# Low parts of attention keys beside rows of zeros: score products over 128 rows instead of 64

## Chip, cores and metric

The kernel runs on one core of a Trainium2 chip, in one launch. The metric is the device time of one execution in microseconds (us). A core has five engines with queues of their own that run in order: TensorE (PE, with its weight loader PEld), VectorE (DVE), ScalarE (ACT), GpSimd (POOL) and SyncE (SP, which issues the transfers).

## What is computed

A network for 256 tokens of width 1024, in float32. Block one has two layers of feed-forward, token mixing, feed-forward; block two has two layers of a hybrid of three attentions followed by an MLP. The change touches two kinds of scores. In token mixing, families A (banded attention) and C (stick-breaking attention), six heads each:

```
scores = jnp.einsum('bnqhd,bnkhd->bhnqk', qc, kband) * (d ** -0.5)     # A, d = 64
z = jnp.einsum('bqhd,bkhd->bhqk', q[:, q0:kend], k[:, :kend]) * scale  # C, d = 64
```

In the hybrid, sparse attention ("nsa") with eight heads in two groups, over compressed, selected and window keys:

```
s_c = jnp.einsum('bgrqd,bgnd->bgrqn', qb, k_cmp)
s_s = jnp.einsum('bgrqd,bgqnld->bgrqnl', qb, k_g)
p_w = masked_softmax(jnp.einsum('bgrqd,bgkd->bgrqk', qb, kwb), mask_w)
```

## The kernel before

Float32 accuracy is reached with split operands: x = H + L, where H is x rounded to the TensorE's fast float32 format and L the rest. A product of two split operands is H·H + H·L + L·H. The weights stream through three raw tiles; ACT writes H, DVE (POOL when DVE is behind) writes L into a ring of six tiles `hl`, and the TensorE takes them from there. The stages run one after the other: feed-forward, mixing, feed-forward for each layer, then hybrid and MLP for each layer. Attention work is laid into the same queues between the weight products.

The order on every engine is fixed when the program is built. `Sched` keeps a clock per engine from a cost per instruction and always issues the instruction that could start first; a task (a generator) waits for tiles from pools (`Slots`) or for flags. A matmul's cost there includes a model of the TensorE's activity, which counts columns times rows (`cols` in `mm`, L546 is the line at which all instructions are issued). All records of the trace therefore carry line L546; instructions are told apart by their tiles.

The scores of a head have 64 rows of contraction (the head's width), half of the 128 rows of the array. Two heads share a tile: head 0 on rows 0 to 63, head 1 on rows 64 to 127. `qk_post` writes for each head x a query tile with H of the query on its own rows and L on the other half, and a key tile `kst` of three planes: plane x has H of the key on all 128 rows, and plane 2 has L of both keys, each on its own rows. `scores` then makes two products per head and token tile: one over 128 rows (H and L of the query times H of the key), and one over 64 rows (H of the query times L of the key):

```
yield self.mm(o, q[:, i, c], k[:, i], seg == 0, False, ...)
yield self.mm(o, q[r, i, c], k[r, 2], False, True, ...)
```

Family C adds the mask with a product by the identity (`identb`, `cb`, bfloat16). In block two `keys` and `nsa_pair` do the same with `kc` (tile `kcat`, H) and `kl` (L, in the place of tile `tA`); `qT` lies in `hlq`. Per layer there are 4 pairs of heads, 2 groups and 3 pairs of products. `nsa_qk` sets the columns behind the keys to zero, `nsa_pair` reads gates from `gate24`. The memory attention (`mem_head`, tiles `hlk` and `hlq`) has heads of 128, so its three products per score are over 128 rows.

Of the kernel before, what the change touches and what calls it, by code (L numbers as in the profile page):

```python
# [45 lines left out]
# ---------------------------------------------------------------- weights  # L46
# The main stream reads the weights in the order of use, in "halves":
# [128, 1024] float32, what one step multiplies with all 256 tokens.

def ws_half(w, c0):  # L50
    """Columns c0:c0+128 of a [1024, n] matrix: [128 p, 8 k, 128 c]."""
    return w[:, c0:c0 + 128].reshape(8, 128, 128).transpose(1, 0, 2).reshape(128, 1024)


def ts_halves(w, cols, per=2):
    """Columns of a [1024, n] matrix, per row chunks of 128 in a half: [128 p, per, n]."""
    a = w[:, cols]
    n = a.shape[1]
    a = a.reshape(8 // per, per, 128, n).transpose(0, 2, 1, 3).reshape(8 // per, 128, per * n)
    if per * n < 1024:  # L60
        a = np.concatenate([a, np.zeros((8 // per, 128, 1024 - per * n), np.float32)], -1)
    return list(a)
# [59 lines left out]
def merge_order(b):  # L122
    """Gates (None, j) and branch halves (i, None) of a branch."""
    if b == 0:
        return [(None, j) for j in range(8)] + [(i, None) for i in range(4)]
    return [u for i in range(4) for u in ((None, 2 * i), (None, 2 * i + 1), (i, None))]
# [56 lines left out]
# ---------------------------------------------------------------- constants of the shapes  # L183
# [9 lines left out]
def constants():  # L193
# [25 lines left out]
    # decay sums: E[tok] = sum over a range of tokens, as columns of 0 or -1/16  # L219
# [10 lines left out]
    # order F, 1, 2, 4, B, 64, 32, 16, 8  # L230

    # predicates for A^T[j, i] of the levels that are computed whole: i = j, and 1, 2, 4, 8
# [13 lines left out]
def prepare(inp, stages):  # L246
# [15 lines left out]
    # block two: per-partition columns of gains, and rows that are broadcast  # L262
# [13 lines left out]
# ---------------------------------------------------------------- the kernel  # L276

class Slots:
    """Tiles that are handed out and returned; a task yields (slots) or (slots, n) to get some."""
# [23 lines left out]
class Op:  # L303
    """One instruction, not yet issued."""
# [12 lines left out]
def region(a):  # L317
    """(name, in PSUM, partitions, elements of a partition) that an operand covers; whole banks of PSUM."""
# [28 lines left out]
class Engine:  # L347
    """Makes the instructions of one engine."""
# [58 lines left out]
class Sched:  # L407
    """Lists the instructions of all tasks in one order: the one that can start first by the engines'
    clocks is issued first. A task is a generator of instructions (Op), of conditions to wait for
    (a function) and of requests for tiles (Slots, or (Slots, n))."""  # L410
# [19 lines left out]
    def step(self, t):  # L430
        """Runs a task up to its next instruction, or until it has to wait."""
# [54 lines left out]
    def stream(self, s, cost, cols):  # L486
        """The end of a matmul that starts at s: the array runs at half its clock in a period that follows
        one of little activity."""
# [120 lines left out]
class Prog:  # L609
# [41 lines left out]
    # ---- small helpers  # L651
# [21 lines left out]
    def mm3(self, out, l, r, start=True, stop=True):  # L673
        """Product of split operands: l(hl), r(hl) give the parts."""
# [6 lines left out]
    def gain(self, ap):  # L681
        """A gain [1024] on every partition, in a scratch tile."""
        g = yield self.scr
        yield self.bcast(g, ap, D)
        return g
# [5 lines left out]
    def hl_gain(self, H, L, src, g):  # L691
        """Split of src * g, g a column or a number."""
# [3 lines left out]
    def chunk(self, src):  # L696
        """A split [128, 256] operand for the main stream."""
# [4 lines left out]
    # ---- weights: loaded and split ahead of the main stream  # L702
# [45 lines left out]
    def pooled(self, low):  # L748
        """Takes what the vector engine falls behind with."""
# [22 lines left out]
    # ---- norms  # L772
    def rstd(self, st, a, b, n):
        """(sum of columns a and b of st + n eps)^-0.5, in place of a."""
# [5 lines left out]
    def norm(self, t, x, Gn, dst, st):  # L780
        """dst[:, k, t, hl, :] = rms(x) * gain of token tile t, transposed and split. Gn: the gain times 32."""
# [31 lines left out]
    # ---- matrix products of the main stream  # L813
    def ws_mm(self, p, w, act, nk=8, off=0, parts=1):
        """Weights stationary. One part: [128 columns, 256]; two, which value() adds: [128 columns, t, hl, 128]."""
# [19 lines left out]
    def ws_first(self, n, done):  # L835
        """The first n products of a stage: those of the first tile of tokens ahead of the others."""
# [23 lines left out]
    def ws_unit(self, parts=1):  # L860
        """One product of the main stream: (result, where it goes back to, parts)."""
# [6 lines left out]
    def value(self, pr):  # L868
        """A product as one [128, 256] operand, and the tile that holds it if there is one."""
# [19 lines left out]
    def ts_bank(self, y, w, c, t, first, last, **kw):  # L889
        """y += tokens of tile t times a chunk w(hl) of weights; c: [128, t, hl, 128]."""  # L890
# [3 lines left out]
    def ts_mm(self, y, w, c, t, first):  # L894
        """y [128, 2, 512] += tokens of tile t times w [128, 1024]."""
# [4 lines left out]
    def ts_group(self, width, split=False):  # L900
        """All tokens times a group of columns: a pair of banks, tokens of a tile in each."""
# [22 lines left out]
    # ---- the end of a stage: the last chunks, residual, next norm  # L924
    def gains(self, post, after):
        """The gains for the end of a stage: that of its result, times 32 and the residual's factor, and the next one's, times 32."""
# [9 lines left out]
    def finish(self, chunks, names, ys, post, after, fills):  # L936
        """The last chunks (by name) of a stage; ys: the banks of the tiles of tokens."""
# [63 lines left out]
    def give_gain(self, name):  # L1001
        """Both tiles of tokens are through with a gain."""
# [5 lines left out]
    # ---- memory: keys and values of both layers, in the gaps between the stages  # L1008
# [16 lines left out]
    def fill(self, f):  # L1025
        """256 columns of the memory's keys (f%4 < 2) or values."""
# [22 lines left out]
    def mem_keys(self, l, c, p, y):  # L1049
        """Normed keys of two heads, transposed: memk[:, head, memory token]."""  # L1050
# [17 lines left out]
    # ---- the feed-forward networks  # L1068
# [71 lines left out]
    # ---- token mixing of block one  # L1140
# [15 lines left out]
    def table(self, name):  # L1156
        """The functions of the next stage, once this one's are done with."""
# [3 lines left out]
    def qk_post(self, l, it, pr, qk):  # L1161
# [9 lines left out]
        else:  # L1171
            # of each of two heads: queries with the high parts on its rows and the low ones on the others;
            # keys with the high parts on all rows, and the low ones on its own
# [4 lines left out]
            for r, o, x in HALVES:  # L1178
                yield nc.vector.scalar_tensor_tensor(t2[r, 2] if what == "k" else t2[o, x], src[r], sc,
# [49 lines left out]
    def scores(self, s, q, k, rows, stacked, strict=False):  # L1229
        """s: a bank [128 q, (q1: 256 keys | q0: 256 keys)] for each of two row groups."""  # L1230
        for i, r in enumerate(rows):
            for seg, t in ((0, 1), (1, 0)):
                o = s[i][:, seg * 256:(seg + 1) * 256]
                c = slice(t * 128, (t + 1) * 128)
                if stacked:
                    yield self.mm(o, q[:, i, c], k[:, i], seg == 0, False, skip_group_check=seg > 0)
                    yield self.mm(o, q[r, i, c], k[r, 2], False, True, skip_group_check=seg > 0)
# [7 lines left out]
    def smax(self, Pt, s, biases):  # L1245
        """Exponentials of biased scores of two maps: P [128, 2, 384], and their sums in st[:, :, 2:4]."""
# [15 lines left out]
    def pv_t(self, Tt, Ps):  # L1262
        """Transposed probabilities [128 k, n, (k0: q0 q1 | k1: q1)] of maps [128 q, (q1: k0 k1 | q0: k0)]."""
# [14 lines left out]
    def pv_mm(self, p, T, col):  # L1278
        """o^T [128 = 2 heads x 64, 256 tokens]; V columns col, col+64."""
# [38 lines left out]
    def att_b(self, j, q, k):  # L1318
# [33 lines left out]
        # r = (mean of the squares of a head + eps)^-0.5 on every partition of the head  # L1352
# [42 lines left out]
    # ---- block two  # L1395
    def setup2(self, p2):
# [12 lines left out]
        self.gate24 = t2([128, 2, 24], "gate24")  # L1409
# [17 lines left out]
    def rope_tables(self):  # L1427
        nc, a = self.nc, self.a
        # cos and sin of position * frequency: [128, 3, 8] (two token tiles, block ends)
# [24 lines left out]
    def again(self, tag, shape, dt=FT):  # L1454
        """A new tile in the place of the last one of a tag."""
# [7 lines left out]
    def rope(self, x, cos, sin, shape):  # L1463
        """Rotates the first 16 of the last axis of x [.., 64] in place."""
# [18 lines left out]
    def head_norm(self, x, p, nt, nh, d, gs, times=1.0):  # L1483
        """x [p, nt, nh, d] in place: rms over d, gains (view of x, gain) or none, times a factor."""
# [59 lines left out]
    def cmp_post(self, v, pr):  # L1544
        """The windows of compressed keys or values: 2 x 16 positions of each, split."""
# [55 lines left out]
    def hyb(self, l, after, fills):  # L1601
        nc, a = self.nc, self.a
        self.done &= {"dec"}
        self.tA, self.tB = (self.again(n, [128, 2, w])[:, :, :512] for n, w in (("tA", 512), ("tB", 768)))
# [4 lines left out]
        # gates, low-rank gate, memory queries, gla values  # L1609
# [27 lines left out]
        # merge  # L1637
# [39 lines left out]
    # ---- memory attention  # L1677
# [60 lines left out]
    # ---- gated linear attention  # L1738
    def gla_gate(self, l):
        """sp = -log sigmoid of the gates, per token, split: [128 tokens, hl, t, 256]."""  # L1740
# [27 lines left out]
    def gla(self):  # L1768
        nc, gq, gr, gv = self.nc, self.gq, self.gr, self.tB
        och = self.och[1] = {}  # L1770
        for half in range(2):
# [6 lines left out]
            for t in range(2):  # L1778
# [14 lines left out]
                # slots: t0: 1 2 4 B | 64 32 16 8, t1: F 1 2 4 | 64 32 16 8  # L1793
# [36 lines left out]
            # o [tokens, dv] of both heads, normed, then transposed  # L1830
# [41 lines left out]
    # ---- nsa: queries, keys, then the three branches  # L1872
    def nsa_qk(self):
# [17 lines left out]
        # of a row group g: rows 64g.. the high parts, the other rows the low parts  # L1891
# [14 lines left out]
        kl = self.again("tA", [128, 2, 512], FR).rearrange("p a c -> p (a c)")[:, :528]  # L1906
        yield nc.vector.memset(kc[:, :, 256:272].bitcast(FT), 0.0)
        yield nc.vector.memset(kl[:, 256:272].bitcast(FT), 0.0)
# [14 lines left out]
    def split_v(self):  # L1923
        yield lambda: ("o", 1) in self.done
        # a token tile, kind: 64 values of the first group, zeros, 64 of the second
# [7 lines left out]
    def keys(self, src, view):  # L1933
        """The high parts of the keys of a row group on all rows, and the low parts on its own."""
# [4 lines left out]
        for r, o, x in HALVES:  # L1939
            yield nc.vector.tensor_sub(view(kl[r]), src[r], view(kc[r, x]).bitcast(FT))  # L1940

    def cmp_tail(self, v, pb):
        """Compressed keys or values: gelu, second product, and for keys norm, rotation, transposition."""
# [47 lines left out]
    def nsa_pair(self, j, qT, kv, och):  # L1991
        """Heads j and j+4 (rows 0-63 and 64-127)."""
# [203 lines left out]
```

## Time and profile before

| | |
|---|---|
| median of 3 runs | 2043.14 us (2041.13 to 2045.71) |
| profiled execution: span, first to last instruction | 2040.8 us |
| own time of the profiled execution | not listed apart from the three runs; its span lies 2.3 us below their median |
| TensorE busy | 1995.6 us, 98% |
| weight loads busy | 1732.3 us, 85% |
| DVE, ACT, POOL busy | 1424.7 us (70%), 1205.0 us (59%), 267.7 us (13%) |
| mean granted TensorE clock | 0.994 |
| transfers | 353.77 MB, mean 173 GB/s |

Busy is the share of time in which an engine has an instruction in flight. TensorE's matmuls overlap: one starts while the one before is still in flight, and ends are modelled. How fast they run is therefore read from the starts, in the timeline: the start of a group, the start of the next, and the count between them. In the names, `b<-kst,qk 64*128 64x256` is a product into a bank `b` of a key `kst` and a query `qk`, weights 64 rows by 128 columns, moving operand 64 rows by 256 columns. PEld rows are the loads of the weights.

### The profile page before, as it was taken

The page shows a single profiled execution, that of the slowest core. Times are in us where ns is not written, and L with a number is a line of the kernel's source. Part 1 is how long each engine was busy: PE and PEld are TensorE (multiplying, and loading weights), DVE is VectorE, ACT ScalarE, POOL GpSimd, SP SyncE. Part 2 cuts the span into 40 slices and gives each one's busy share as a digit, 9 for nine tenths or more (in the row PEclk, how much of TensorE's full clock was granted, in tenths as well). Part 3 has the DMA queues.
Part 4 walks back from the last instruction along what each step waited for, and adds up shares of the span by engine and source line. Part 5 has one row for each costly group of instructions (what it writes and reads, how often), then busy time and mean ns, then how long its engine had stood idle before and what let it go on. Part 6 is the DMA issues. An engine that isn't in the chain of part 4 may idle for free. (4 is left out here: it accounts for less than half of the span.)

```text
span 2040.8 us, 31877 instructions
## 1 busy us (share of the span) xinstructions
PE 1995.6 (98%) x11942; PEld 1732.3 (85%) x11942; DVE 1424.7 (70%) x2525; ACT 1205.0 (59%) x2328; POOL 267.7 (13%) x311
## 2 busy tenths in 40 slices
PE   8999999999999999999999999999999999999999
PEld 7888777888888887788889888998888978898887
DVE  6666887666776678776668777666667787667665
ACT  6655775655565568665556656655555656655553
POOL 1000302000200030020003132310001232411000
PEclk9999999999999999999999999999999999999999
DMA  6655344655665644455565544355565544335553
GB/s 218 222 192 199 117 152 146 215 193 188 208 198 192 206 156 135 167 176 190 187 206 193 173 146 135 102 167 183 192 198 189 165 148 142 114 130 191 188 194 124
DMA packets 100561, 353.77 MB, mean 173 GB/s; under 512 B 12435, under 2 KB 13493, under 8 KB 100406
## 3 DMA queue, kind: packets, MB, share of 16 engines
q1 hardware_dynamic: 100406, 351.74, 52.2%
q8 instruction: 93, 1.52, 0.3%
q14 instruction: 62, 0.51, 0.1%
HBM read 350.64 MB, written 1.05 MB: 172 GB/s over the span
## 5 line engine op out<-in xcount | busy, mean ns | idle before, releaser
L546 PE MATMUL m<-hT,hl 128*128 128x256 f32 (+1 forms) x5856 | 976.4, 322 | 7.7 <-DVE hT L546 7.0
L546 PEld LDWEIGHTS m<-hT,hl 128*128 128x128 f32 x5856 | 853.6, 189 | 104.1 <-DVE hT L546 9.6
L546 ACT CAST hl<-raw 128x1024 fp32r<-128x1024 f32 (+1 forms) x690 | 671.4, 982 | 380.3 <-PE b L546 141.3
L546 DVE TENSOR_TENSOR hl<-raw,hl 128x1024 fp32r<-128x1024 f32 (+1 forms) x641 | 755.5, 1184 | 200.1 <-ACT hl L546 193.1
L546 PE MATMUL b<-hl,chunk 128*128 128x512 f32 x2208 | 517.0, 390 | 0.0
L546 PEld LDWEIGHTS b<-hl,chunk 128*128 128x128 f32 x2208 | 408.9, 188 | 81.8 <-issue 0.7
L546 DVE TENSOR_TENSOR mid<-m,lo 128x256 f32<-128x256 f32 x256 | 108.5, 424 | 221.8 <-ACT lo L546 221.3
L546 PE MATMUL b<-hl,hT 128*128 128x512 f32 (+2 forms) x672 | 149.4, 371 | 0.5 <-DVE hT L546 0.5
L546 ACT CAST chunk<-mid 128x256 fp32r<-128x256 f32 x152 | 61.7, 406 | 120.8 <-DVE mid L546 120.4
L546 POOL TENSOR_SCALAR scr<-scr 128x1024 f32<-128x1024 f32 x17 | 21.1, 1239 | 834.9 <-DMA scr<-ffn_post_g 451.6
L546 PEld LDWEIGHTS b<-hl,hT 128*128 128x128 f32 x672 | 115.9, 188 | 16.6 <-DVE hT L546 0.8
L546 POOL TENSOR_TENSOR hl<-raw,hl 128x256 fp32r<-128x256 f32 x104 | 103.0, 1017 | 192.0 <-ACT hl L546 155.1
L546 ACT COPY lo<-m 128x256 f32<-128x256 f32 x256 | 95.0, 371 | 23.8 <-PE m L546 22.7
L546 PE MATMUL b<-ident,scr 128*128 128x128 f32 (+2 forms) x458 | 78.3, 284 | 17.8 <-DVE scr L546 14.0
L546 PE MATMUL m<-chunk,hl 128*128 128x256 f32 x576 | 82.4, 292 | 0.0
L546 PEld LDWEIGHTS b<-ident,scr 128*128 128x128 f32 (+2 forms) x458 | 54.3, 143 | 33.0 <-DVE scr L546 20.3
L546 PEld LDWEIGHTS m<-chunk,hl 128*128 128x128 f32 x576 | 74.3, 195 | 3.0 <-ACT scr L546 0.7
L546 ACT ACTIVATE scr<-scr,sts 128x16 f32<-128x16 f32 (+2 forms) x152 | 62.8, 415 | 9.4 <-DVE sts L546 9.1
L546 DVE TENSOR_TENSOR chunk<-mid,chunk 128x256 fp32r<-128x256 f32 x152 | 65.3, 430 | 2.3 <-ACT chunk L546 2.0
L546 POOL TENSOR_SCALAR scr<-scr,sts 128x128 f32<-128x128 f32 (+2 forms) x96 | 55.9, 602 | 79.3 <-DVE sts L546 52.1
L546 ACT COPY scr<-b 16x16 f32<-16x16 f32 (+6 forms) x148 | 35.4, 239 | 41.2 <-PE b L546 33.5
L546 ACT ACTIVATE mid<-mid 128x256 f32<-128x256 f32 x88 | 36.7, 417 | 34.1 <-DVE mid L546 34.1
(204 smaller groups left out, 1622.4 us busy)
## 6 DMA issues: line engine op xcount, KB each, us to landing
raw<-w SPq DMA_DIRECT2D x636, 512.0 KB, 3.4
scr<-mem SPq DMA_DIRECT2D x4, 512.0 KB, 6.2
scr<-ffn_post_g SPq DMA_DIRECT2D x4, 512.0 KB, 5.0
bias<-bias SPq DMA_DIRECT2D x6, 256.0 KB, 3.6
scr<-ffn_pre_g SPq DMA_DIRECT2D x3, 512.0 KB, 5.9
scr<-mem_norm SPq DMA_DIRECT2D x2, 512.0 KB, 4.9
scr<-mix_pre_g SPq DMA_DIRECT2D x2, 512.0 KB, 4.2
bias<-alibi SPq DMA_DIRECT2D x4, 256.0 KB, 4.3
```

The costliest lines, as they stand in the source:

```text
L546: r = op.call(*op.args, **op.kw) if op.call is not None else None
```

## The change

Each head gets a plane for the low parts of its key as wide as the array: L on the head's own rows, zeros on the other half. The low product then takes the whole query tile (H and L) and this plane; L of the query meets the zeros. The value is the same. In block one the key tile has four planes instead of three, and there are three such tiles instead of four; the zero halves are written once, at the start, on POOL, and stay. In block two `kl` gets a plane per group (528 columns each) and is set to zero as a whole by DVE at the place where 16 columns were. The tile `tA` grows from 512 to 528 columns a plane, and `gate24` becomes the first 24 columns of `gl` instead of a tile of its own. Comments are gone too, so line numbers move.

```diff
@@ qk_post
             for r, o, x in HALVES:
-                yield nc.vector.scalar_tensor_tensor(t2[r, 2] if what == "k" else t2[o, x], src[r], sc,
+                yield nc.vector.scalar_tensor_tensor(t2[r, 2 + x] if what == "k" else t2[o, x], src[r], sc,
                                                      t2[r, x].bitcast(FT), op0=OP.mult, op1=OP.subtract)
@@ scores
                     yield self.mm(o, q[:, i, c], k[:, i], seg == 0, False, skip_group_check=seg > 0)
-                    yield self.mm(o, q[r, i, c], k[r, 2], False, True, skip_group_check=seg > 0)
+                    yield self.mm(o, q[:, i, c], k[:, 2 + i], False, True, skip_group_check=seg > 0)
@@ setup2
-        self.gate24 = t2([128, 2, 24], "gate24")
+        self.gate24 = self.gl[:, :, 0:24]
@@ hyb
-        self.tA, self.tB = (self.again(n, [128, 2, w])[:, :, :512] for n, w in (("tA", 512), ("tB", 768)))
+        self.tA, self.tB = (self.again(n, [128, 2, w])[:, :, :512] for n, w in (("tA", 528), ("tB", 768)))
@@ nsa_qk
-        kl = self.again("tA", [128, 2, 512], FR).rearrange("p a c -> p (a c)")[:, :528]
+        kl = self.again("tA", [128, 2, 528], FR)
         yield nc.vector.memset(kc[:, :, 256:272].bitcast(FT), 0.0)
-        yield nc.vector.memset(kl[:, 256:272].bitcast(FT), 0.0)
+        yield nc.vector.memset(kl.bitcast(FT), 0.0)
@@ keys
-            yield nc.vector.tensor_sub(view(kl[r]), src[r], view(kc[r, x]).bitcast(FT))
+            yield nc.vector.tensor_sub(view(kl[r, x]), src[r], view(kc[r, x]).bitcast(FT))
@@ nsa_pair
                 yield self.mm(u[:, :n], qT[:, g, j, tq], kc[:, g, c:c + n], True, False)
-                yield self.mm(u[:, :n], qT[r, g, j, tq], kl[r, c:c + n], False, True)
+                yield self.mm(u[:, :n], qT[:, g, j, tq], kl[:, g, c:c + n], False, True)
@@ main
-                self.kst = Slots(p1, "kst", 4, [128, 3, 256], FR)
+                self.kst = Slots(p1, "kst", 3, [128, 4, 256], FR)
...
+                for t in self.kst.free:
+                    for r, o, x in HALVES:
+                        yield nc.gpsimd.memset(t[o, 2 + x].bitcast(FT), 0.0)
```

The order of the instructions on TensorE, at the first scores of family A (`kst` is the key tile, `qk` the query, `b` the bank; - is before, + is now; sizes are those of the results):

```order
 L546 MATMUL m_64<-hT,hl_96 128x2x128
 L546 MATMUL m_63<-hT,hl_97 128x512 x7
-L546 MATMUL b_65<-kst_142,qk_134 128x256 x4
-L546 MATMUL b_70<-kst_142,qk_134 128x256 x4
+L546 MATMUL b_65<-kst_139,qk_134 128x256 x4
+L546 MATMUL b_70<-kst_139,qk_134 128x256 x4
 L546 MATMUL m_63<-hT,hl_97 128x512
 L546 MATMUL m_63<-hT,hl_97 128x2x128 x8
```

The eight products stand where they stood; only the key tile is another of the pool. It is so in all of TensorE's queue. On POOL, at the start of the program (`small` holds the sums for the first norm):

```order
+L546 MEMSET kst_139 64x256 x2
+L546 MEMSET kst_140 64x256 x2
+L546 MEMSET kst_141 64x256 x2
 L546 ISA
 L546 TENSOR_TENSOR small_108<-small_108,mhalf 128x1
```

Six memsets are new ahead of POOL's first work. On DVE, in the sparse attention of the first layer (`hlq` queries, `kcat` and `tA` keys, `hl` a weight half):

```order
 L546 TENSOR_TENSOR hlq<-b_65,hlq 64x512 x2
 L546 MEMSET kcat 128x2x16
-L546 MEMSET tA 128x16
+L546 MEMSET tA 128x1056
 L546 TENSOR_TENSOR hl_96<-raw_95,hl_96 128x1024
 L546 TENSOR_TENSOR tA<-b_66,kcat 64x15 x2
```

The memset keeps its place and grows.

## Rows read from the trace of the kernel before

**Rows 1.** The page: TensorE's busy time, and its clock in 40 slices.

```profile
PE 1995.6 (98%) x11942; PEld 1732.3 (85%) x11942; DVE 1424.7 (70%) x2525; ACT 1205.0 (59%) x2328; POOL 267.7 (13%) x311
PEclk9999999999999999999999999999999999999999
```

**Rows 2.** Stretches: us, then each engine's busy time (instructions), clock, DMA share, GB/s.

```profile
223.00:258.00 35.00, 35.00 (x203) 28.69 (x202) 28.66 (x47) 29.76 (x57) 0.00 (x0) 1.00 0.44 146
285.00:325.00 40.00, 40.00 (x204) 30.59 (x202) 30.05 (x86) 28.42 (x71) 0.59 (x3) 1.00 0.49 162
1238.00:1274.00 36.00, 34.56 (x255) 30.27 (x253) 26.89 (x95) 25.01 (x81) 11.83 (x20) 1.00 0.38 131
```

**Rows 3.** TensorE's waits, 223 to 325, then 1238 to 1310: total us, times, longest.

```profile
PE b L546 <- DVE chunk L546: 1.0, 1, 1.0
...
PE b L546 <- POOL scr L546: 1.4, 1, 1.4
```

**Rows 4.** Groups by shape, products, then loads: count, busy us, mean ns, idle before.

```profile
L546 PE MATMUL b<-kst,qk 64*128 64x256 f32 x48 | 18.3, 381 | 0.0
L546 PE MATMUL b<-kst,qk 128*128 128x256 f32 x48 | 17.0, 355 | 0.0
...
L546 PEld LDWEIGHTS b<-tA,hlq 64*128 64x128 f32 x48 | 8.8, 183 | 6.4 <-issue 0.2
```

**Rows 5.** Timeline of TensorE from 286 us (family A): start us, us, what, count.

```profile
286.06 2.10 PE L546 MATMUL m<-hT,hl 128*128 128x256 f32 x8
287.99 2.47 PE L546 MATMUL b<-kst,qk 128*128 128x256 f32 x8
290.39 0.50 PE L546 MATMUL m<-hT,hl 128*128 128x512 f32 x1
```

**Rows 6.** Timeline of TensorE from 1120.5 us: scores of the memory attention.

```profile
1120.98 1.84 PE L546 MATMUL b<-hlk,hlq 128*128 128x256 f32 x14
1122.66 0.51 PE L546 MATMUL m<-hT,hl 128*128 128x256 f32 x3
```

**Rows 7.** Timeline of the weight loads from 286 us; [idle before <- released by].

```profile
286.03 1.69 PEld L546 LDWEIGHTS m<-hT,hl 128*128 128x128 f32 x8
287.76 0.19 PEld L546 LDWEIGHTS b<-kst,qk 128*128 128x128 f32 x1
288.20 2.06 PEld L546 LDWEIGHTS b<-kst,qk 64*128 64x128 f32 x7 [0.25 <-issue]
```

**Rows 8.** Timeline of TensorE from 1257 us, behind scores of the sparse attention.

```profile
1257.83 2.88 PE L546 MATMUL m<-hT,hl 128*128 128x256 f32 x22
1260.55 0.64 PE L546 MATMUL m<-chunk,hl 128*128 128x256 f32 x4
```

**Rows 9.** Timeline of TensorE from 229.2 us (family C): a mask product and its successor.

```profile
232.50 0.28 PE L546 MATMUL b<-cb,identb 128*128 128x256 bf16 x1
232.54 0.72 PE L546 MATMUL m<-hT,hl 128*128 128x512 f32 x3
```

**Rows 10.** Timeline of POOL: its first work, and a memset in the mixing stage.

```profile
5.96 0.56 POOL L546 TENSOR_TENSOR small<-small,mhalf 128x1 f32<-128x1 f32 x1 [5.52 <-DVE small L546]
...
303.00 0.20 POOL L546 MEMSET bias<- 64x128 f32 x1 [8.18 <-DMA bias<-bias]
```

**Rows 11.** Timeline of DVE from 1238 us: the memset and what follows.

```profile
1238.75 0.07 DVE L546 MEMSET tA<- 128x16 f32 x1
1238.85 1.23 DVE L546 TENSOR_TENSOR hl<-raw,hl 128x1024 fp32r<-128x1024 f32 x1
...
1240.32 0.36 DVE L546 TENSOR_TENSOR tA<-b,kcat 64x15 fp32r<-64x15 f32 x2 [0.24 <-ACT kcat L546]
...
1242.09 1.72 DVE L546 COPY_PREDICATED scr<-pred,b 128x128 f32<-128x128 uint8 x5 [1.42 <-ACT scr L546]
```

**Rows 12.** Timeline of ACT: writes of the first and the fourth key.

```profile
227.33 0.42 ACT L546 ACTIVATE kst<-mid 64x256 fp32r<-64x256 f32 x1
...
282.60 0.42 ACT L546 ACTIVATE kst<-mid 64x256 fp32r<-64x256 f32 x1
```

More of the change, by code (lines that the diff above doesn't have):

```diff
@@ L1999, in nsa_pair @@
         for g in range(2):
-            r = HALVES[g][0]
             sb = yield self.b, 3
```

## Prediction

> **What bounds the kernel now.** I read the page first. TensorE is busy 98% of the span and its granted clock stands at nine tenths or more of the upper level (2.4 GHz) in all 40 slices [rows 1], so only time taken off TensorE's own queue, or off its few waits, can shorten the run. Then the table by stretches, laid over the two places where the changed products run: the mixing stages of block one, at 223 to 325 us and again at 756 to 858, and the sparse attention of block two, at 1238 to 1310 and again at 1716 to 1788. There TensorE is full, at an undisturbed clock of 1.00; the next engines, ACT and DVE, stand at 29.76 and 28.66 of 35 us in the tightest stretch [rows 2]. Third, who waits: in the whole first mixing stage TensorE waits 1.0 us (for DVE), in one sparse attention 1.4 us (for POOL) [rows 3]. So TensorE is the bound in both places, with ACT close behind it at 85%.
>
> Last, the instructions themselves. "Busy" says nothing about the speed of one product, because TensorE's rows overlap; the distance from start to start does. A block of eight score products runs from 287.99 to 290.39: 2.40 us, 0.300 us each [rows 5]. The closest relative with all 128 rows in every operand, the score products of the memory attention (also split in three, also 256 columns, also into one bank), runs 14 products from 1120.98 to 1122.66: 0.120 us each [rows 6]. The weight loads say why. While products of 128 rows follow each other, each load is made while the product before it still runs: eight loads from 286.03 to 287.76, beside the eight products from 286.06 to 287.99 [rows 5, 7]. At the step from a load of 128 rows to one of 64 rows the loader stands still for 0.25 us and is released by nothing that the profile shows [rows 7]. Each block alternates between 128 and 64 rows, so it pays this at every product. That is the stall which the change can take away: not the half-empty array, but the alternation.
>
> **The change, part by part.**
>
> (1) *Widened products.* No product is added or taken away; on TensorE the order is the same and only names of key buffers differ. 96 products of 64 rows (48 in block one, 48 in block two [rows 4]) become products of 128 rows. Each narrow product has two borders, one into it and one out of it. Price of a border: the block of eight has eight (four in, four out). It costs 2.40 us against 8 x 0.120 = 0.96, so 1.44 too much. The bill doesn't end with the block: the first product behind it has a late load too. Behind a block in block two, 22 products take 1257.83 to 1260.55 = 2.72 us instead of 22 x 0.120 = 2.64 [rows 8], 0.08 more. So 1.52 us for eight borders, 0.19 us each. 192 borders x 0.19 = 36.5 us. One correction: the 12 mask products (bfloat16, one per head of family C and layer), which stand behind narrow ones, are followed after only 0.04 us [rows 9] where a plain product takes 0.12; so 12 x 0.08 = 1 us of the border is not there to be saved. That leaves 35.5 us, all on TensorE's own queue, where nothing hides it. Bounds for a widened product, which the trace of before does not show: 0.120 us (the relative) and 0.300 us (as now). I take the relative, since it is the same operation at the same width.
>
> The Trainium skill has a rule that would speak against this. Its page "TensorE: Matmul & The Clock Gate", section "Part 3: Packing small matmuls — row/col tiling", says that a weight load overlaps a running product only where the two use different row groups; by that rule widening would make every load collide and the saving would be nothing (a rival below). The trace disagrees for full rows: the loads of 128 rows above keep up with products of 128 rows.
>
> (2) *What is late next.* A faster TensorE asks for its operands sooner. In the stretch 223 to 258 about 12 narrow products give back 24 x 0.19 = 4.6 us less 0.5 us for six masks, 4.1 us; TensorE then needs 30.9 us and ACT 29.8, 96%. I let 1 us of that be lost in each of the two layers. In 285 to 325 TensorE goes from 40.0 to 35.4 and DVE stays at 30.1: covered. In block two TensorE gives back 48 borders x 0.19 = 9.1 us a layer out of 72; DVE is at 26.9 of 36 and ACT at 25.0, both covered, but the one wait for POOL (1.4 us) can grow, since less work stands between scores and the transposes behind them. I let 0.5 us be lost per layer. Sum of the losses 2 x 1 + 2 x 0.5 = 3 us.
>
> (3) *Zeros for block one.* Six memsets of 64x256 on POOL at the start. A memset of 64x128 took 0.20 us [rows 10], so 0.40 each, 2.4 us in all (bounds 0.2 and 2.4). They stand at the head of POOL's queue, whose first work begins at 5.96 us after an idle time of 5.52 us. Hidden; without that cover 2.4 us, once.
>
> (4) *Zeros for block two.* DVE's memset before the keys grows from 16 to 1056 columns, twice in the run. 16 columns took 0.07 us; an operation of 1024 columns on DVE at this place takes 1.23 us [rows 11]. Between these I take 0.9 us. Behind it stand one weight half and the low parts of the keys; just before and after these DVE waits 0.24 and 1.42 us for ACT, which takes up the 0.9 [rows 11]. Cost nothing; without that cover 2 x 0.9 = 1.8 us.
>
> (5) *Three key tiles in place of four.* The first of a stage's keys is written from 227.33 us on and the fourth from 282.60 [rows 12]. With three tiles the fourth takes the first one's place, and the first one's scores end with the mask product at 232.50 [rows 9], 50 us before. Nothing. The gates that move into another tile's columns keep their operations and their order: nothing. (The lower bound of (3) to (5) is nothing, since none of them takes work away.)
>
> **Sum.** 35.5 - 3 = 32.5, rounded to 32 us. The profiled execution spans 2040.8 us, the median of the runs is 2043.1; the 2.3 us around the span I leave as they are. 2043.1 - 32 = 2011 us.
>
> **Rivals.**
>
> A. *The other engines take over.* The borders vanish, but ACT's in-order queue in block one and the chain scores, DVE, ACT, POOL, transposes in block two already pace the work. For it: ACT at 85%, the wait for POOL. Against it: TensorE waits only 1.0 and 1.4 us in 100 and 72 us. Then 223 to 258 gives nothing (2 x 4.1 = 8.2 lost) and each of the four head pairs of a layer in block two loses what one block of six saves, 6 x 0.19 = 1.1 us (8 x 1.1 = 9 lost): gain 35.5 - 17 = 18, time 2025.
>
> B. *No gain: it is not the row count.* The loader's 0.25 us could belong to something else that score products share, say that every load collides with the product before it in the same rows, or two products into one bank. For it: the profile names no releaser. Against it: the memory attention has all of this and runs at 0.120. Time 2043, within 2 us. This is where the page's rule would lead.
>
> C. *Slower: rows cost array time.* A product's time could grow with its rows; then 96 products take twice their 0.12 us, and where blocks border on other narrow work the stall stays. It decides once a widened product passes the 0.300 us of now: 96 x 0.12 = 11.5 us more and no stall saved, 2055. Against it: nothing in the profile makes a 128-row product longer than a 64-row one; the modelled durations are 0.355 and 0.381 us, the other way round [rows 4].
>
> **How the numbers follow.** Forecast 0.80, A 0.14, B 0.03, C 0.03. The forecast's own spread: with no loss to other engines and the waits of 1.0, 1.4 and 1.4 us gone as well it is 35.5 + 4 = 40 less, 2003; losing a further 5 us gives 2016. The range takes in A, whose centre is 2025, up to 2026. 0.2% is 4.1 us, about what separates a real difference from none here. Forecast and A lie beyond it, with a small part of A short of it: faster 0.94. B is "same": 0.03. C: 0.03 slower.
>
> **What would show it.** In the profile after, no load of 64 rows for these keys; a block of eight score products in about 0.96 us, with no still loader inside it; TensorE's instruction count as before and its total busy time some 30 us lower; each mixing stage about 7 us and each sparse attention about 8 us shorter, everything else the same length. If a block is that short but the stage is not, A holds, and TensorE's waits for ACT, DVE or POOL in it show where. If the blocks stay at 2.4 us, B. The forecast is wrong as a mechanism if the saving lies in other stages or in the clock.

## The result and the profile after

The changed kernel takes 2015.38 us (median of 4 runs, 2013.92 to 2016.40), beside 2044.24 us for the kernel before on the same chip (4 runs): ratio 0.986, 95% interval 0.9846 to 0.9874, that is 28.9 us less. The forecast was 2011 us with a range of 2003 to 2026. The profiled execution spans 2012.0 us against 2040.8; the mean granted clock is 0.993 against 0.994, so the gain does not come from the clock.

The page after has as many products as before, 31.9 us less busy time on TensorE, and six more instructions on POOL [rows 1]:

```profile
PE 1963.7 (98%) x11942; PEld 1724.9 (86%) x11942; DVE 1424.6 (71%) x2525; ACT 1203.0 (60%) x2328; POOL 267.9 (13%) x317
PEclk9999999999999999999999999999999999999999
```

Groups by shape: all 96 products of `kst` now form one group, and no load of 64 rows is left for these keys. The modelled mean fell from 381 and 355 ns [rows 4] to 289, close to the 298 ns of the memory attention's products:

```profile
L546 PE MATMUL b<-kst,qk 128*128 128x256 f32 x96 | 16.0, 289 | 0.0
L546 PE MATMUL b<-tA,hlq 128*128 128x272 f32 x32 | 9.5, 296 | 0.0
...
L546 PEld LDWEIGHTS b<-kst,qk 128*128 128x128 f32 x96 | 14.1, 190 | 1.2
L546 PEld LDWEIGHTS b<-tA,hlq 128*128 128x128 f32 x48 | 9.1, 189 | 0.0
```

The first block of family A, which took 2.40 us [rows 5], in the timeline of TensorE (start us, us, what, count):

```profile
283.64 2.10 PE L546 MATMUL m<-hT,hl 128*128 128x256 f32 x8
285.57 1.12 PE L546 MATMUL b<-kst,qk 128*128 128x256 f32 x8
286.53 3.67 PE L546 MATMUL m<-hT,hl 128*128 128x512 f32 x21
```

and in that of its weight loads, where the still loader of [rows 7] is gone:

```profile
283.61 1.69 PEld L546 LDWEIGHTS m<-hT,hl 128*128 128x128 f32 x8
285.35 1.14 PEld L546 LDWEIGHTS b<-kst,qk 128*128 128x128 f32 x8
286.41 3.69 PEld L546 LDWEIGHTS m<-hT,hl 128*128 128x128 f32 x22
```

From start to start the block now takes 286.53 - 285.57 = 0.96 us, 0.120 us each. The loads run without a gap beside the products.

The stretches that answer to [rows 2] (same columns; they begin earlier because the run is ahead):

```profile
222.00:252.00 30.00, 29.58 (x197) 26.42 (x196) 25.26 (x44) 27.57 (x54) 0.14 (x1) 1.00 0.40 134
280.00:318.00 38.00, 38.00 (x223) 31.20 (x221) 32.25 (x91) 30.55 (x78) 0.59 (x3) 1.00 0.53 173
1224.00:1254.00 30.00, 28.16 (x241) 27.18 (x240) 25.32 (x82) 22.89 (x77) 10.46 (x17) 1.00 0.41 140
```

In the first and the third stretch nearly as many products now pass in 30 us as in 35 or 36 before; ACT, at 27.57 of 30 us, has come close to TensorE in the first stretch. TensorE's waits in the first mixing stage (223 to 318 us), then in the first sparse attention (1224 to 1290), against 1.0 and 1.4 us [rows 3]:

```profile
PE b L546 <- ACT scr L546: 2.1, 1, 2.1
PE m L546 <- DVE mid L546: 0.4, 1, 0.4
...
PE b L546 <- POOL scr L546: 1.4, 1, 1.4
PE m L546 <- DVE hlk L546: 0.4, 1, 0.4
```

The order on TensorE is the same in both kernels, so each distance from one product's start to the next can be set against the same distance before. Summed by stage, the distances around the changed products (the one into each group of them, those inside, and the two behind) are shorter by 8.6 us in each mixing stage and by 8.8 us in each sparse attention: **34.8 us**. All other distances in the same stages are longer by 1.9, 2.5, 0.7 and 0.7 us: **5.8 us given back**. The rest of the run comes to 0.3 us more. Together 28.7 us less, beside 28.8 as the difference of the spans. (The expectations below price a border at 0.178 us, from 33.4 us. That sum leaves out the distance into each group, where 0.44 us a mixing stage and 0.27 us a sparse attention are saved.) What is open after that: whether 64 rows as such or the alternation cost the 34.8 us, and what took 5.8 us back.

### The profile page after: what moved, and what is told of

The parts are those of the page before. It is cut to its first block, busy times and chain, and to the rows that moved or that the text cites. A ratio compares the mean times of both kernels' runs of the same rounds, so it can differ in the third digit from the quotient of the medians.

```text
span 2012.0 us, 31884 instructions
## 1 busy us (share of the span) xinstructions
PE 1963.7 (98%) x11942; PEld 1724.9 (86%) x11942; DVE 1424.6 (71%) x2525; ACT 1203.0 (60%) x2328; POOL 267.9 (13%) x317
```

## The experiments

Each run stands beside runs of the kernel before on its chip: 2044.01 us (9 runs) for the first four, 2044.84 us (9 runs) for the next four, 2044.38 us (10 runs) for the last two. "Distances" are sums of start-to-start distances as above, of one profiled execution each.

**Block one alone.** The kernel before with the change to the mixing stages only:

```diff
-                    yield self.mm(o, q[r, i, c], k[r, 2], False, True, skip_group_check=seg > 0)
+                    yield self.mm(o, q[:, i, c], k[:, 2 + i], False, True, skip_group_check=seg > 0)
...
```

> Only block one's keys (mixing) get planes of zeros; block two is as before. Theory (the alternation between 128 and 64 rows costs, by the border): of the 299 changes of row count in TensorE's queue before, 96 go. The trace of after priced a border at 33.4 us / 188 = 0.178 us, so 17 us come off the score blocks, and 3 to 4 us come back as waits in the mixing stages: 2031 us beside 2044 of before. Rival (the gain is not local to the blocks, for instance a better clock or transfers over the whole run): the share of block one is not tied to its borders; 2015 or 2044 are then as likely as 2031.

Measured: 2032.8 us, ratio 0.9941 [0.9928, 0.9953], 11.2 us less. The distances of the scores fall by 8.6 us in both mixing stages, those of the sparse attention stay (0.01). Other distances of the two mixing stages grow by 2.0 and 2.7 us: this loss belongs to this part.

**Block two alone.** The other hunks on the kernel before:

```diff
-                yield self.mm(u[:, :n], qT[r, g, j, tq], kl[r, c:c + n], False, True)
+                yield self.mm(u[:, :n], qT[:, g, j, tq], kl[:, g, c:c + n], False, True)
...
```

> Only block two's keys (sparse attention) get planes of zeros; block one is as before. Theory: 92 borders go, 16.4 us off the blocks, about 1 us back: 2028.5 us beside 2044, and its gain and that of block one alone add up to that of the whole change (28.9). Rival (not local): as for block one alone, and the two gains don't add up.

Measured: 2028.28 us, ratio 0.9926 [0.9912, 0.9939], 15.7 us less. The distances of the scores fall by 8.8 us twice, 0.7 us come back in each layer. The two parts add up to 26.9 us against 28.9 for the whole: within the spread of the runs they are independent.

**Nothing widened, alternation halved.** The kernel before; the low products keep their 64 rows, but each run of products H L H L is put in the order H H L L, in the same places:

```diff
+    def regroup(self, ops):
...
+        real = [(p.args, p.kw) for p in ops[0::2] + ops[1::2]]
+        for p, (p.args, p.kw) in zip(ops, real):
+            yield p
...
```

> Nothing is widened: low products keep their 64 rows. Within a head's scores the products over 128 rows now stand first and those over 64 rows behind them, at the places of the old order. 100 of 299 borders go. Theory (alternation): 17.8 us off the blocks, about 2.5 us back: 2029 us beside 2044, with 48 + 48 narrow products still there. Rival (a product over 64 rows is slow by itself, full rows make it fast): no change, 2044, within 4 us.

Measured: 2026.11 us, ratio 0.9916 [0.9903, 0.993]. With all 96 narrow products still narrow, 17.9 of 28.9 us are gained. In the sparse attention of this kernel three products of 64 rows in a row run like any other; only the steps in and out cost:

```profile
1248.54 0.53 PE L546 MATMUL b<-kcat,hlq 128*128 128x272 f32 x3
1248.99 0.64 PE L546 MATMUL b<-tA,hlq 64*128 64x272 f32 x3
1249.56 0.63 PE L546 MATMUL m<-hT,hl 128*128 128x256 f32 x3
```

Six products take 1.02 us for 6 x 0.12 = 0.72 of plain work. In the kernel before they took 1.79 us, from the start of this product to the 1257.83 us of [rows 8]:

```profile
1256.04 0.28 PE L546 MATMUL b<-kcat,hlq 128*128 128x272 f32 x1
```

In TensorE's order one can count the places at which the rows change (32, 64 or 128; 48 rows go with 64): 299 in the kernel before, 199 here, 111 in the changed kernel. The distances of the scores fall by 19.2 us for 100 changes, **0.19 us each**; in the changed kernel by 34.8 us for 188, **0.19 us each** (0.185). One price fits both, and in one of the two kernels nothing is widened: what costs is the step between row counts, not the count.

**All score products narrow.** The kernel before; the high products lose half of their rows, so that H and L both have 64 (the product of the low query with the high key is left out):

```diff
-                    yield self.mm(o, q[:, i, c], k[:, i], seg == 0, False, skip_group_check=seg > 0)
+                    yield self.mm(o, q[r, i, c], k[r, i], seg == 0, False, skip_group_check=seg > 0)
@@ nsa_pair
-                yield self.mm(u[:, :n], qT[:, g, j, tq], kc[:, g, c:c + n], True, False)
+                yield self.mm(u[:, :n], qT[r, g, j, tq], kc[r, g, c:c + n], True, False)
```

> The other way round: the high products are narrowed to 64 rows too (high part of the query times high part of the key; the product of the query's low part and the key's high part is left out), so all 192 score products are narrow. 80 of 299 borders go, 6 new steps between the two row halves come. Theory (alternation): 14.2 us off the blocks, 2 us back: 2032 us beside 2044; inside a run of narrow products 0.12 us from start to start. Rival (full rows make a product fast): each of 192 narrow products costs 0.30 us: 96 x 0.18 = 17 us slower than before, 2061.

Measured: 2026.1 us, ratio 0.9912 [0.9898, 0.9925], 5.9 us better than the 2032 expected. Some 3.3 us of this are family A's: each of its six narrow blocks saves 1.62 us with the steps into and out of it, where six borders less at 0.178 us would be 1.07. These blocks are even faster than wide ones:

```profile
285.26 2.10 PE L546 MATMUL m<-hT,hl 128*128 128x256 f32 x8
287.30 0.74 PE L546 MATMUL b<-kst,qk 64*128 64x256 f32 x8
287.97 3.33 PE L546 MATMUL m<-hT,hl 128*128 128x512 f32 x17
```

Eight products take 0.67 us, 0.084 us each, below the 0.120 of the full-row score products. Head 0's four, on rows 0 to 63, stand ahead of head 1's four, on rows 64 to 127, in the queue; yet the starts lie in pairs 12 to 15 ns apart. In the trace the first low product of each head, which carries a wait, is the second and the sixth of the eight to start in the kernel before, and the third and the fourth here. So a product of one half starts beside one of the other half, ahead of its turn: unlike what the first section says of all queues, TensorE does not start products strictly in order when they use different halves. In the sparse attention the product with the compressed values (rows 0 to 47) stands in the queue behind four score products of the second half, and starts beside the first of them:

```profile
1291.12 0.39 PE L546 MATMUL b<-kcat,hlq 64*128 64x272 f32 x1
1291.13 0.48 PE L546 MATMUL b<-mid,vcmp 48*128 48x256 f32 x1
```

Where the six products of a run use the same half and nothing narrow stands behind them, they are 0.12 us apart as usual:

```profile
1245.58 0.39 PE L546 MATMUL b<-kcat,hlq 64*128 64x272 f32 x1
1245.81 0.29 PE L546 MATMUL b<-tA,hlq 64*128 64x272 f32 x1
1245.94 0.28 PE L546 MATMUL b<-kcat,hlq 64*128 64x256 f32 x1
1246.06 0.27 PE L546 MATMUL b<-tA,hlq 64*128 64x256 f32 x1
```

except the first, at the step into them (0.23). The stall stands at the step between row counts, whichever way the rows are made equal. Rival B, that something else in these products causes it, falls.

**Low products over 96 rows.** The changed kernel; the low products of head 0 and of group 0 take 96 of the 128 rows, the rest being zeros anyway:

```diff
-                    yield self.mm(o, q[:, i, c], k[:, 2 + i], False, True, skip_group_check=seg > 0)
+                    yield self.mm(o, q[:128 - 32 * (i == 0), i, c], k[:128 - 32 * (i == 0), 2 + i], False, True, skip_group_check=seg > 0)
...
```

> The changed kernel, but the low products of head 0 and of group 0 (half of the 96) take 96 rows: the head's own 64 and 32 of the 64 rows of zeros. The result is the same. Theory (what costs is a change of the array's row division, 32, 64 or 128, and 96 rows need the one of 128): no border comes back, 2015 us as after, within 3. Rival (only operands that fill all 128 rows are loaded early, or any change of the row count costs): the borders of 48 products come back, 94 x 0.178 = 17 us: 2032.

Measured: 2015.06 us, ratio 0.9861 [0.9845, 0.9877], as the changed kernel. 24 products of `kst` have 96 rows now, and nothing returned:

```profile
L546 PE MATMUL b<-kst,qk 128*128 128x256 f32 x72 | 15.1, 293 | 0.0
...
L546 PE MATMUL b<-kst,qk 96*128 96x256 f32 x24 | 6.3, 282 | 0.0
```

The distances of the scores move by 0.06 us at most in a stage. So not every other row count costs: 96 stands with 128, 64 and 48 do not.

**The values' product over 128 rows.** The changed kernel still has narrow neighbours in the sparse attention: the product with the compressed values has 48 rows. Here it gets 128 (zeros behind):

```diff
-        self.vcmp = t2([48, 128], "vcmp")
+        self.vcmp = t2([128, 128], "vcmp")
...
-            yield self.tr(p[:48, 128 * t:128 * t + 128], pc[:, t, 0:48])
+            yield self.tr(p[:, 128 * t:128 * t + 128], pc[:, t])
```

> The changed kernel, and the same means at another place: the product of compressed values and probabilities in the sparse attention (48 rows, 8 of them) gets rows of zeros up to 128. 16 of the 111 borders that are left go. Theory: 16 x 0.178 = 2.8 us less than the changed kernel, 2012.5. Rival (the wider transposes and the larger memset on POOL in front of it lie on the chain scores, POOL, transposes and eat it): 2015 or more.

Measured: 2013.14 us (2011.11 to 2019.15), ratio 0.9852 [0.9833, 0.9871]. The sparse attentions of the profiled execution are 1.2 and 1.3 us shorter, 2.5 in all for 16 changes less (0.16 each). But 3.2 and 2.5 us went the other way in its mixing stages, which this edit doesn't touch: the granted clock was 0.97 and 0.98 there, and 1.00 in both stages of the changed kernel's profiled execution. The interval holds the changed kernel's 0.986: not to be told from no gain by its time.

**The zeros of block two on POOL.** The changed kernel; the memset of 1056 columns goes from DVE to POOL, to see whether it causes the new wait of 0.4 us for DVE's `hlk`:

```diff
-        yield nc.vector.memset(kl.bitcast(FT), 0.0)
+        op = nc.vector.memset(kl.bitcast(FT), 0.0)
+        op.call = nc.gpsimd._r.memset
+        yield op
```

> The changed kernel with the zeros of block two written by POOL instead of DVE, at the same place of the order. Theory (the 0.94 us on DVE are not hidden in full: behind them TensorE waits 0.4 us for DVE's hlk in each layer, which it didn't before): 0.5 to 1 us less than the changed kernel, 2014.5, and the wait for DVE's hlk gone from the trace. Rival (hidden, the wait has another cause): 2015 and the wait still there. Time alone can't tell these apart; the wait in the trace does.

Measured: 2017.14 us, ratio 0.9866 [0.9849, 0.9883]. The wait is still there:

```profile
PE b L546 <- POOL scr L546: 1.4, 1, 1.4
PE m L546 <- DVE hlk L546: 0.4, 1, 0.4
```

The memset isn't its cause, and taking it off DVE shows no gain.

**Both of these.** The last two edits in one kernel:

```diff
+        self.vcmp = t2([128, 128], "vcmp")
...
+        op.call = nc.gpsimd._r.memset
```

> The changed kernel with both additions: the values' product over 128 rows, and block two's zeros on POOL. Theory: the two gains add, 2.8 + 0.7 us less than the changed kernel: 2012, beside 2044 of before. Rival (POOL becomes late, since it now writes all zeros of block two at the start of the pairs' chain): 2015 or more, with TensorE's wait for POOL above 1.4 us.

Measured: 2012.31 us (2008.50 to 2012.69), ratio 0.9839 [0.9824, 0.9855]: the lowest median of a kernel that computes everything, 3 us below the changed kernel, but the intervals overlap, and the mean granted clock of its profiled execution was 0.996 against 0.993. TensorE's wait for POOL stayed at 1.4 us. The sparse attentions are again 1.2 and 1.3 us shorter; that part is seen twice.

**Half of each weight transfer, changed kernel.** In the trace after, TensorE's wait of 2.1 us leads to ACT. ACT's queue at that place:

```profile
253.88 1.03 ACT L546 CAST hl<-raw 128x1024 fp32r<-128x1024 f32 x1
258.10 1.04 ACT L546 CAST hl<-raw 128x1024 fp32r<-128x1024 f32 x1 [3.19 <-DMA raw<-w]
259.05 0.84 ACT L546 ACTIVATE scr<-scr 128x768 f32<-128x768 f32 x1
```

and the same place in the kernel before:

```profile
256.39 1.03 ACT L546 CAST hl<-raw 128x1024 fp32r<-128x1024 f32 x1
258.88 1.05 ACT L546 CAST hl<-raw 128x1024 fp32r<-128x1024 f32 x1 [1.46 <-DMA raw<-w]
259.83 0.84 ACT L546 ACTIVATE scr<-scr 128x768 f32<-128x768 f32 x1
```

ACT got here 2.5 us earlier but the weights only 0.8 us earlier, so a cast of weights holds ACT for 3.19 us instead of 1.46, and the exponential of the scores stands behind it. To test this, each weight transfer after the third brings half of its columns, with every order as it was:

```diff
+            op = self.nc.sync.dma_start(t, self.a["w"][i])
+            if i >= 3:
+                op.args = (t[:, :512], self.a["w"][i][:, :512])
+            yield op
```

> The changed kernel, but each weight transfer after the third brings only half of its columns (the other half of the raw tile keeps older weights, so the values are left out of the comparison); the order on every engine stays. It tests where the 4 us came from that the mixing stages gave back. Theory (the late weight transfer holds up a cast on ACT, and the exponential behind it, and so TensorE): the waits of 2.1 us (mixing of layer one) and 1.1 us (mixing of layer two) of TensorE for ACT's scores go, the two mixing stages are together 2 to 4 us shorter than in the changed kernel, about 2011 to 2013 us for the run if nothing else waits for transfers. Rival (ACT's own work is the pace, with or without the transfer): the waits stay at 1 us or more in each stage and the time at 2015.

Measured: 2007.47 us, ratio 0.9817 [0.9803, 0.983]. In TensorE's timeline of this kernel the transposes now follow the products without a wait:

```profile
251.72 3.42 PE L546 MATMUL b<-hl,hT 128*128 128x512 f32 x14
255.10 0.55 PE L546 MATMUL b<-ident,scr 128*128 128x128 f32 x3
```

The changed kernel at the same place, with the wait in brackets:

```profile
251.81 6.05 PE L546 MATMUL b<-hl,hT 128*128 128x512 f32 x25
259.94 0.33 PE L546 MATMUL b<-ident,scr 128*128 128x128 f32 x1 [2.08 <-ACT scr L546]
```

The distance at this step is 2.12 us shorter than in the changed kernel and that at the same step of the second layer 1.15 us; the mixing stages together are 4.3 us shorter, somewhat more than expected. The run as a whole came out 3.5 us below the expected 2011 to 2013: 2.7 us more were saved ahead of the first mixing stage, which the theory did not name. All that is left of TensorE's waits in them is 0.2 us each. The rival, ACT's own pace, falls for these two steps: ACT has the same work.

**Half of each weight transfer, kernel before.** The same edit on the other side:

> The kernel before with the same halved weight transfers (half of each weight's columns left out after the third). Theory: the kernel before waits little for its transfers (1.0 us in mixing of layer one, 0.2 in layer two), so 2042 to 2044 us, and the difference to the changed kernel with halved transfers is 30 to 33 us, more than the 28.8 us with full transfers, because none of it is given back in the mixing stages. Rival (the pace of ACT itself): the difference stays at 28 to 29 us.

Measured: 2038.23 us, ratio 0.9973 [0.9961, 0.9984]. It fell by 6 us where 0 to 2 were expected; of this 1.6 us are in the first mixing stage and 0.9 before it, and part of the rest is a stretch whose mean granted clock was higher in this execution (1.00 against 0.99 between 1310 and 1716 us). The difference between the two halved kernels is 2038.23 - 2007.47 = **30.8 us**, against 28.9 with full transfers and within the 30 to 33 that the theory expected; but each of the two ratios is known to some 0.0013 only, 2 to 3 us, so these times alone don't tell 30.8 from 28.9. The traces do: the scores gain the same 8.6, 8.6, 8.8 and 8.8 us, and the mixing stages give back 0.9 us each in place of 1.9 and 2.5. So 2.7 of these 4.4 us are due to the transfers.

## Why the prediction was right

The cause, the place and the sign were as forecast, and the time lies 4.4 us above the forecast. The gain of the products had nearly the forecast size; the losses behind it were about twice the forecast ones. Point by point:

1. *The bound and the stall.* TensorE's queue was the bound in both places, and the alternation of 128 and 64 rows was the stall: a block fell to 0.96 us as forecast, the order H H L L gains most of it without a widened product, and products that are all narrow gain it too. The rate of the memory attention [rows 6] was the right end of the bounds 0.120 and 0.300.
2. *The size of term (1).* Forecast 35.5 us, measured 34.8. The price was right: 0.19 was forecast, 0.185 measured. The count was too high by 4: I gave each narrow product two borders of its own, but 188 changes of row count vanish in TensorE's order, not 192, since some narrow products stand next to others (those of 48 rows). In block two that is 46 changes a layer at 8.8 us, 0.19 each. In block one 48 changes give 8.6 us, 0.18 each, as expected with the 0.5 us a layer that I took off for the mask products.
3. *What is late next, term (2).* Forecast 3 us, measured 5.8: this is the term that was mis-sized. In block two I said 0.5 us a layer and 0.7 were lost, but not where I said: the wait for POOL stayed at 1.4 us [rows 3], and a wait for DVE's `hlk` is new, in a place where I had called DVE covered. DVE's own queue is the cause. In the kernel before, DVE was done with a weight half and then stood idle until TensorE had finished the product that `hlk` is read from:

```profile
1249.13 1.22 DVE L546 TENSOR_TENSOR hl<-raw,hl 128x1024 fp32r<-128x1024 f32 x1
1251.29 0.42 DVE L546 SCALAR_TENSOR_TENSOR hlk<-scr,m 128x256 f32<-128x256 f32 x1 [0.93 <-PE m L546]
```

   After, TensorE has gained 2.3 us in the score groups just ahead of this place, more than the 0.93 us; DVE goes from the weight half to `hlk` without a pause, and TensorE waits for it:

```profile
1235.16 1.22 DVE L546 TENSOR_TENSOR hl<-raw,hl 128x1024 fp32r<-128x1024 f32 x1
1236.30 0.41 DVE L546 SCALAR_TENSOR_TENSOR hlk<-scr,m 128x256 f32<-128x256 f32 x1
1236.77 2.05 PE L546 MATMUL m<-hT,hl 128*128 128x256 f32 x15 [0.40 <-DVE hlk L546]
```

   In block one I said 1 us a layer, and 1.9 and 2.5 us were lost. I had named ACT by its share of 96% in one stretch. The longest wait is for ACT, but not because ACT is full: it stands idle for a weight transfer, with the scores' exponential behind that in its queue. With halved transfers 1.1 and 1.6 us of the loss go and 0.9 us a stage stays. The transfers are the step that I left out; [rows 2] showed their share at 0.44 to 0.49, which said nothing about when one lands.
4. *Zeros and tiles, terms (3) to (5).* POOL's six memsets take 2.04 us (2.4 forecast), and its first work behind them begins at 5.72 us, where it was 5.96 in the kernel before [rows 10]:

```profile
0.73 2.04 POOL L546 MEMSET kst<- 64x256 f32 x6 [0.29 <-POOLq L2190]
5.72 0.56 POOL L546 TENSOR_TENSOR small<-small,mhalf 128x1 f32<-128x1 f32 x1 [2.95 <-DVE small L546]
```

   DVE's memset takes 0.94 us (0.9 forecast) at this place [rows 11], and its removal gained nothing:

```profile
1224.98 0.94 DVE L546 MEMSET tA<- 128x1056 f32 x1 [0.17 <-issue]
1225.95 1.22 DVE L546 TENSOR_TENSOR hl<-raw,hl 128x1024 fp32r<-128x1024 f32 x1
```

   Three key tiles in place of four make no wait: ACT, which writes a key first, stands idle ahead of that only for DVE's `mid`, in four places as before, and never for the scores that used the tile.
5. *The sum.* 34.8 - 5.8 = 29.0, where 35.5 - 3 = 32.5 had been forecast: 0.7 us from the first term, 2.8 from the second. Rival A had the direction of the second, and its mechanism is at work in block two, but it put the loss at 17 us against 5.8; rival C is ruled out by the block of 0.96 us.
6. *The rule weighed against the change.* By a bullet of the section "Part 3: Packing small matmuls — row/col tiling" of the Trainium skill's page "TensorE: Matmul & The Clock Gate", a weight load overlaps products only in other row groups. The loads of the changed block, all on the same 128 rows, run beside its products at 0.120 us each: for full rows the trace still disagrees. What the runs fit is a sentence of the Trainium skill's page "TensorEngine Tiling (Array Packing)", section "Key Properties": a change of the tiling mode, unlike a change of the tile, drains TensorE. The runs show the price of a step between row counts, about 0.19 us, and not the draining itself; steps between the two halves of the array cost nothing in them (the block of 0.67 us).

A mixing stage's loss is not of one execution alone. Where the granted clock stood at 1.00 through the stage, the first stage with widened products gave back 1.7 to 2.0 us in three executions, the second 2.1 to 3.0 us in five. In other executions the clock fell within such a stage (0.97 in the first one of the kernel with low products of 96 rows) and the stage gave back more; that the changed kernel's profiled execution, the fastest of its four, had 1.00 in both is luck.

Open: why the waits of a mixing stage fall on ACT in some executions and on DVE in others, and what the 0.9 us a stage are that stay with halved transfers. In the kernel with the 128-row values, the wait at 257 us was gone and another of 1.5 us for DVE stood further on.

## What to carry to other kernels

Look in the timeline for neighbours on TensorE whose row counts fall on different sides of the line between 64 and 96, and count the changes in the instruction order: each cost 0.16 to 0.19 us here, more than the 0.12 us of a product. Padding with zeros, or putting equal ones side by side, takes them away; the second is free and alone gave 62% of the gain (17.9 of 28.9 us). When a full queue gets faster, look not only at the busy shares of the other engines but at what stands in their queues ahead of the needed instruction: here a cast that waited for a transfer, and on DVE a weight half ahead of the operation that frees TensorE's bank.

## What the hardware showed beyond that

- Narrow products on the two halves of the array run at the same time: eight of 64 rows in 0.67 us, where eight of 128 rows take 0.96. They do so even when all of one half stand behind those of the other in the queue. On one half alone they are as slow as full ones (0.12 us each).
- A product of 96 rows next to one of 128 costs nothing (score distances within 0.06 us a stage).
- A step between row counts costs about the same for 64 rows beside 128 (0.19 us, H H L L) as for 48 beside 128 (2.5 us for 16 changes, 0.16 us).
- Halving all weight transfers is worth 6 to 8 us of some 2,000, though the transfers' mean busy share is about one half: in the changed kernel's traces 4.3 us of it lie in the mixing stages and 2.7 us ahead of the first.
